# Hyena filters with a tile of taps per direction, and their transform taken from sums and differences

## The chip, the cores and the metric

The kernel runs on one core of a Trainium2 chip. The number that counts is the device time of one execution, in microseconds. The core has a matrix engine (TensorE, PE in the profile; PEld is its loading of weights), three engines for elementwise work (VectorE is DVE, ScalarE is ACT, GpSimd is POOL), and DMA queues, nearly all of which are issued here from SyncE (SP). Each engine works through its own list of instructions in order; semaphores tie the lists together.

## The reference, cut to what matters

The program is a two-layer backbone on 1024 latent tokens with 256 context tokens: an attention layer, then a layer of gated long convolutions (Hyena). All is float32. The change touches only the Fourier transforms of the convolution filters, which don't depend on the tokens:

```python
def hyena_filters(L, w1, b1, w2, b2, w3, b3, freq):
    ...
    hid = jnp.sin(_f32(freq) * (emb @ _f32(w1) + _f32(b1)))
    hid = jnp.sin(_f32(freq) * (hid @ _f32(w2) + _f32(b2)))
    h = (hid @ _f32(w3) + _f32(b3)).reshape(L, HY_ORDER, 2, HY_WIDTH)
    ...
    h = h * jnp.exp(-t * jnp.abs(deltas))[:, None, None, :]
    fwd, bwd = h[:, :, 0], h[:, :, 1]
    kern = jnp.concatenate([fwd, jnp.zeros((1, HY_ORDER, HY_WIDTH), jnp.float32), bwd[:0:-1]], axis=0)
    kern = kern / jnp.sum(jnp.abs(kern), axis=0, keepdims=True)
    return jnp.fft.rfft(kern, axis=0)
```

L is 1024, so a filter has 2048 taps: 1024 forward ones, a zero and 1023 backward ones. There are 2 orders of 1024 channels. A tap is a product of 64 hidden values with w3 and a bias b3, times a decay; a filter is divided by the sum of its absolute taps; its spectrum is wanted.

## The kernel before, in words

The filters are made in the first 250 us, ahead of and beside the preparation of the tokens. Channels are taken in 8 blocks (p) of 128, each with both orders, so 256 columns (CB). The 2048 taps of a block come in 16 tiles (g) of 128 rows, four tiles per step: `steps` lists 32 steps (p, gq), with gq from 3 down to 0, and one loop over n from 0 to 37 (line 605) issues, in this order:

- `taps(n)`, PE. A product in float32 is made of three in the faster fp32r form, with each factor split in a high and a low part (`mm3`, lines 100 to 103). For each of the four tiles, one matmul adds the bias (`ind` times `b4`, line 480) and three do the product of hidden values and w3 (`Hh`, `Hl` with `w3h`, `w3l`). The 64 hidden values of a forward row and of a backward row share the 128 rows of a tile, with zeros in the half that isn't theirs.
- `decay(n + 1)`, ACT: the decays of the next step (line 531).
- `second_stage`, PE (line 573): the second half of an earlier block's transform, in two halves, ps0 and ps1, each with `spectra` on DVE (line 584), which scales it by 1 / norm and sends it to DRAM (`Kd`). Tile `kc`, which it writes, has two buffers.
- `decayed(n)`, DVE (line 536): taps out of PSUM times decay into the tile `kern` of 128x1024 (two buffers).
- `first_stage(n - 1, j)`, j = 0 and 1: the first half of the transform, one float32 matmul of 128x512 on PE with the constant `FK` (line 558), and a copy by ACT into `aT` (line 560). So it works one step behind.
- `norms(n)`: ACT takes absolute values, in two pieces of 512 columns (line 545), and POOL adds them to `kacc` (line 547).
- `regroup`: four DMAs that turn `aT` into `au`, rows for the second stage.
- `split_coefs(p + 1)` once per block: w3 and b3 of the next block in high and low parts, by ACT, POOL and DVE (lines 336 to 345); `coefs` loads them.
- `pull(mods)`, `pull(stats)`, `pull(toks, 2)`: the work of other parts, threaded into the loop. Up to n = 11 `stats` gives ACT a square of a token tile (line 381). From n = 11 on `toks` prepares tokens: PE transposes four blocks (line 409), ACT scales them into `mraw` (line 414), DVE casts the high parts (line 421), POOL subtracts for the low parts (line 422), and in every second step DVE scales the next token tile `xt` (line 403).

This order is the order of each engine's list. PSUM is handed out by rotation: `pw` has two buffers for the taps, `pq` walks over three banks and from n = 20 over four, and whoever takes a bank waits for the reader of what was in it.

After n = 37 the input projection of the attention layer follows on the same engines.

Of the kernel before, what the change touches and what calls it, by code (L numbers as in the profile page):

```python
# [109 lines left out]
def backbone(tc, I, out):  # L110
# [200 lines left out]
    Hh = fp.tile([P, 16, P], F32R, tag="Hh", name="Hh")  # L311
    Hl = fp.tile([P, 16, P], F32R, tag="Hl", name="Hl")
    ind = fp.tile([P, P], F32R, tag="ind", name="ind")
    FKc = fp.tile([P, P], F32, tag="FK", name="FKc")
# [21 lines left out]
    def split_coefs(p):  # L336
        w3r, b3r, dl = coef[p]
        w3h = fp.tile([P, CB], F32R, tag="w3h", bufs=2, name=nm("w3h"))
        w3l = fp.tile([P, CB], F32R, tag="w3l", bufs=2, name=nm("w3l"))
        nc.scalar.copy(w3h, w3r)  # L340
# [2 lines left out]
        nc.scalar.copy(b4[0:2], b3r)
# [92 lines left out]
    with tc.manual_schedule(engines=ENG):  # L436
# [36 lines left out]
        def taps(n):  # L473
            p, gq = steps[n]
            w3h, w3l, b4, _ = coef[p]
            pws[n] = pw()
            for i in range(4):
                g = 4 * gq + i
                pv = pws[n][:, i * CB:(i + 1) * CB]
                nc.tensor.matmul(pv, ind, b4, start=True, stop=False)  # L480
# [1777 lines left out]
```

## Time and profile before

| | |
|---|---|
| median of 3 runs | 1850.01 us (1847.22 to 1852.31) |
| profiled execution | 1850.4 us, of which its span 1848.5 us |
| granted TensorE clock, mean | 0.986 |
| PE busy | 1744.1 us (94%) |
| DVE, ACT, POOL busy | 1136.7, 749.9, 866.2 us |
| `decayed(0)`, `decayed(12)`, `decayed(31)` start | 30.54, 100.50, 223.25 us |
| projection's first cast on ACT | 251.80 us |

The times of `decayed` on DVE (line 536) mark the steps of the loop, and are used as its milestones below: step n begins where `decayed(n)` starts. A row of the timeline gives the start, the time taken, the engine, the line, what is written and read, and how many instructions were put together; in brackets stands how long the engine was idle before it and what ended that. A group's row gives the total busy time and the mean of one in ns. A line's or tile's row gives the least, the median and the longest time of one.

### The profile page before, as it was taken

Reading aid. Unit: us, or ns where it says so; the run is one execution under the profiler, and the core shown is the slowest. Engines: PE = TensorE matmul, PEld = TensorE weight load, DVE = VectorE, ACT = ScalarE, POOL = GpSimd, SP = SyncE. Lnnn points to the kernel's source line nnn. Section 1 sums busy time; section 2 is a strip of 40 time slices with the busy share of each in tenths; the row PEclk is TensorE's granted clock in tenths of the full one; section 3 lists DMA queues with packets and bytes.
Section 4 is the critical chain, followed back from the end, with each engine's and each line's share of the span. In section 5 each row is a group of like instructions: output and inputs, shape, how many; then the busy total and the mean of one; then the engine's idle time right before and its main releaser. Section 6 shows DMA issues by size and latency. Waiting matters only on the chain.

```text
span 1848.5 us, 25379 instructions
## 1 busy us (share of the span) xinstructions
PE 1744.1 (94%) x9360; PEld 1332.5 (72%) x9360; DVE 1136.7 (61%) x1646; ACT 749.9 (41%) x1250; POOL 866.2 (47%) x606
## 2 busy tenths in 40 slices
PE   7899999999999998899999999999999999889898
PEld 2677788977765665565656688888878888778676
DVE  5467657446777877777777423555676666555743
ACT  4878711253544544343443333243333343333332
POOL 2457622443378778566666453234243334334300
PEclk9999999999999999899999999999999999999999
DMA  7776688122120011001000215567778787787623
GB/s 248 231 225 217 201 260 271 56 80 80 36 58 24 13 44 29 27 21 34 19 22 29 77 69 149 166 172 219 219 205 235 227 244 204 204 239 217 202 93 112
DMA packets 243427, 253.18 MB, mean 137 GB/s; under 512 B 28191, under 2 KB 193087, under 8 KB 242887
## 3 DMA queue, kind: packets, MB, share of 16 engines
q1 hardware_dynamic: 241128, 249.47, 45.2%
q10 hardware_dynamic: 2176, 2.10, 0.4%
q8 instruction: 74, 1.21, 0.3%
q14 instruction: 49, 0.40, 0.1%
HBM read 169.65 MB, written 61.94 MB: 125 GB/s over the span
## 4 chain that ended last, share of the span: by engine, by line
PE 54%; DVE 10%; DMA 5%; POOL 2%; ACT 2%; issue 2%; SPq 1%; POOLq 0%; DVEq 0%; ACTq 0%
PE pw L1253 8%; PE pw L103 8%; PE pw L101 8%; PE pw L102 8%; PE pv L1166 6%; PE pq L988 3%; PE pq L101 2%; PE pq L102 2%; PE pq L103 2%; PE pq L1818 2%; DMA K<-Kd 2%; PE pq L1835 2%; DVE mx L989 2%; DMA bd<-cbT 1%; DMA ad<-caT 1%
## 5 line engine op out<-in xcount | busy, mean ns | idle before, releaser
L1261 ACT ACTIVATE PT<-pw 128x1024 f32<-128x1024 f32 x160 | 163.6, 1023 | 218.2 <-PE pw L1253 210.1
L989 DVE TENSOR_REDUCE mx<-pq 128x1 f32<-128x512 f32 (+1 forms) x384 | 215.5, 594 | 42.3 <-PE pq L988 38.7
L101 PE MATMUL pw<-h1h,wh 128*128 128x512 f32 x512 | 209.6, 409 | 0.0
L103 PE MATMUL pw<-h1h,wl 128*128 128x512 f32 x512 | 202.5, 396 | 3.6 <-POOL wl L1676 3.6
L102 PE MATMUL pw<-h1l,wh 128*128 128x512 f32 x512 | 200.8, 392 | 0.0
L1811 POOL TENSOR_TENSOR K<-K,skp 128x512 f32<-128x512 f32 x64 | 85.4, 1336 | 217.7 <-DMA K<-Kd 210.9
L1175 POOL TENSOR_TENSOR acc<-acc,PT 128x1024 f32<-128x1024 f32 x62 | 147.7, 2383 | 35.9 <-ACT PT L1261 33.7
L103 PEld LDWEIGHTS pw<-h1h,wl 128*128 128x128 f32 x512 | 96.5, 188 | 25.7 <-POOL wl L1676 4.3
L1821 DVE SCALAR_TENSOR_TENSOR cB<-pq,K 64x512 f32<-64x512 f32 x64 | 44.3, 693 | 110.6 <-PE pq L1818 36.6
L547 POOL TENSOR_TENSOR kacc<-kacc,kabs 128x512 f32<-128x512 f32 x56 | 72.2, 1289 | 83.8 <-ACT kabs L545 81.9
L102 PEld LDWEIGHTS pw<-h1l,wh 128*128 128x128 f32 x512 | 97.3, 190 | 17.9
L101 PEld LDWEIGHTS pw<-h1h,wh 128*128 128x128 f32 x512 | 97.3, 190 | 17.5
L1173 POOL TENSOR_TENSOR acc<-PT,PT 128x1024 f32<-128x1024 f32 x31 | 73.7, 2377 | 74.3 <-DVE acs L1184 63.7
L1676 POOL TENSOR_TENSOR wl<-wr,wh 128x1024 fp32r<-128x1024 f32 x32 | 78.6, 2455 | 54.5 <-ACT wh L1675 36.2
L1791 ACT COPY caT<-pq 128x512 f32<-128x512 f32 x64 | 37.6, 587 | 142.0 <-PE pq L103 101.9
L1166 PE MATMUL pv<-PT,Va 128*64 128x256 f32 x640 | 86.7, 392 | 2.3 <-DVE gT L1212 2.3
L1166 PE MATMUL pv<-PT,Vm 128*64 128x256 f32 x640 | 85.9, 391 | 0.0
L1852 DVE TENSOR_TENSOR cil<-spare,cih 128x512 fp32r<-128x512 f32 x64 | 57.1, 930 | 42.2 <-ACT cih L1851 42.2
L573 PE MATMUL pq<-au,FBk 128*128 128x256 f32 x256 | 68.3, 391 | 11.8 <-DVE kc L584 11.6
L1818 PE MATMUL pq<-cau,FB 128*128 128x128 f32 x512 | 69.7, 280 | 8.9 <-DVE cA L1824 7.9
L1835 PEld LDWEIGHTS pq<-cA,GB 128*128 128x128 f32 x512 | 67.6, 193 | 12.3 <-issue 7.1
L1837 ACT COPY cbT<-pq 128x512 f32<-128x512 f32 x64 | 37.3, 587 | 95.9 <-PE pq L1835 53.0
(444 smaller groups left out, 4727.1 us busy)
## 6 DMA issues: line engine op xcount, KB each, us to landing
K<-Kd SPq DMA_DIRECT2D x128, 256.0 KB
au<-aT SPq DMA_DIRECT2D x128, 128.0 KB
space<-in_ada_w_dram SPq DMA_DIRECT2D x32, 512.0 KB
wr<-in_hy_w_in_dram SPq DMA_DIRECT2D x32, 512.0 KB
ad<-caT SPq DMA_DIRECT2D x64, 256.0 KB
cau<-ad SPq DMA_DIRECT2D x32, 512.0 KB
bd<-cbT SPq DMA_DIRECT2D x32, 512.0 KB
spare<-bd SPq DMA_DIRECT2D x64, 256.0 KB
```

The lines of the kernel that those rows point to most:

```text
L101: nc.tensor.matmul(ps, lh, rh, start=start, stop=False)
L102: nc.tensor.matmul(ps, lh, rl, start=False, stop=False)
L103: nc.tensor.matmul(ps, ll, rh, start=False, stop=stop)
L989: nc.vector.reduce_max(mxs[gi][:, p:p + 1], ps[:, :w], axis=AX.X)
L1166: nc.tensor.matmul(ps[64 * e:64 * e + 64, 0:256], vals[:, 2 * s + j], PT[:, j, 256 * e:256 * e + 256], start=s == 0 and j == 0, stop=s == ...
L1175: eng.tensor_tensor(accs[gi], accs[gi], PT, ALU.add)
L1253: nc.tensor.matmul(ps[:, 512 * j:512 * j + 512], l[:, kt * P:(kt + 1) * P], r, start=i == 0, stop=i == len(passes) - 1)
L1261: nc.scalar.activation(PT, ps.rearrange("p (a q) -> p a q", q=512), AF.Exp, scale=SC_A if kind == 0 else SC_M)
L1676: nc.gpsimd.tensor_tensor(wl, f(r), f(wh), ALU.subtract)
L1811: nc.gpsimd.tensor_tensor(K[:, 0], K[:, 0], B["skp"].unsqueeze(1).to_broadcast([P, 4, P]), ALU.add)
L1818: nc.tensor.matmul(ps[:, i * P:(i + 1) * P], FB[:, 4 * uc + i, :], au[:, 4 * (uc % 2) + i, :], start=True, stop=True)
L1835: nc.tensor.matmul(ps[:, i * P:(i + 1) * P], GB[:, 4 * uc + i, :], A1[:, i, :], start=True, stop=True)
```

## The change

A tile of taps now holds one direction: `HA` and `HB` are the stationary tiles for direction d and tile g. The 64 rows that held zeros hold the low parts of the hidden values (`HA`), and in `HB`, ones beside the high parts. On the other side `WA` has w3's high part twice, and `WB` w3's low part and the bias with its own low part. Two matmuls for a tile give all four products.

A step still has four tiles, two forward and two backward, so that `kern` has taps n in its first 512 columns and taps n + 1024 in its second 512. A new function `halves` makes their sum (a new tile `sum`, one buffer) and their difference (in place, in the first half), and `first_stage` transforms the sum with one constant matrix for the even frequencies and the difference with another for the odd ones. The numbers and sizes of the matmuls of the two transform stages and of the DMAs of `regroup` stay. `norms` comes in three pieces: two of 256 columns into `kabs` (one buffer now), and one of 512 in place in the second half of `kern`, after `halves` has read it. POOL adds in pieces of 256 columns, four per step. `split_coefs` has six ACT copies instead of two, two POOL subtractions and two DVE ones instead of one each, and stands at the third step of a block instead of the second.

```diff
     def split_coefs(p):
         w3r, b3r, dl = coef[p]
-        w3h = fp.tile([P, CB], F32R, tag="w3h", bufs=2, name=nm("w3h"))
-        w3l = fp.tile([P, CB], F32R, tag="w3l", bufs=2, name=nm("w3l"))
-        nc.scalar.copy(w3h, w3r)
-        nc.gpsimd.tensor_tensor(w3l, w3r, f(w3h), ALU.subtract)
-        b4 = b4s[p % 2]
-        nc.scalar.copy(b4[0:2], b3r)
-        nc.vector.tensor_tensor(b4[32:34], b3r, f(b4[0:2]), ALU.subtract)
+        wa = fp.tile([P, 2, CB], F32R, tag="WA", bufs=2, name=nm("WA"))
+        wb = WB[p % 2]
+        for i in range(2):
+            a = slice(64 * i, 64 * i + 64)
+            for h in (a, slice(64 - 64 * i, 128 - 64 * i)):
+                nc.scalar.copy(wa[h, i], w3r[a])
+            nc.gpsimd.tensor_tensor(wb[a, i], w3r[a], f(wa[a, i]), ALU.subtract)
+            b_ = 64 * (1 - i)
+            nc.scalar.copy(wb[b_:b_ + 1, i], b3r[b_:b_ + 1])
+            nc.vector.tensor_tensor(wb[b_ + 32:b_ + 33, i], b3r[b_:b_ + 1], f(wb[b_:b_ + 1, i]), ALU.subtract)
...
             for i in range(4):
-                g = 4 * gq + i
+                d, g = i // 2, 2 * gq + i % 2
                 pv = pws[n][:, i * CB:(i + 1) * CB]
-                nc.tensor.matmul(pv, ind, b4, start=True, stop=False)
-                mm3(nc, pv, Hh[:, g], Hl[:, g], w3h, w3l, False, True)
+                nc.tensor.matmul(pv, HA[:, d, g], wa[:, d], start=True, stop=False)
+                nc.tensor.matmul(pv, HB[:, d, g], wb[:, d], start=False, stop=True)
...
-            c = slice(8 * q, 8 * q + 8)
-            for h in hs:
-                nc.scalar.activation(Hr[h, c, h], args[q][h, :].rearrange("p (g m) -> p g m", m=64), AF.Sin)
-            nc.scalar.copy(Hh[:, c], Hr[:, c])
-            (nc.vector, nc.gpsimd)[q].tensor_tensor(Hl[:, c], Hr[:, c], f(Hh[:, c]), ALU.subtract)
+            c = slice(4 * q, 4 * q + 4)
+            a = args[q].rearrange("p (g m) -> p g m", m=P)
+            nc.scalar.activation(a, a, AF.Sin)
+            for d, h in enumerate(hs):
+                nc.scalar.copy(HA[h, d, c], a[h])
+                nc.gpsimd.tensor_copy(HB[h, d, c], HA[h, d, c])
+                nc.vector.tensor_tensor(HA[hs[1 - d], d, c], a[h], f(HA[h, d, c]), ALU.subtract)
...
-            for i in range(2):
-                ab = accs[p] if gq == 3 and i == 0 else fw.tile([P, 512], F32, tag="kabs", bufs=2, name=nm("kabs"))
-                nc.scalar.activation(ab, kns[n][:, 512 * i:512 * i + 512], AF.Abs)
-                if ab is not accs[p]:
-                    nc.gpsimd.tensor_tensor(accs[p], accs[p], ab, ALU.add)
...
+            if i == 2:
+                k = ab = kns[n][:, 512:]
+            else:
+                k = kns[n][:, CB * i:CB * i + CB]
+                ab = acc if first else fw.tile([P, CB], F32, tag="kabs", bufs=1, name=nm("kabs"))
+            nc.scalar.activation(ab, k, AF.Abs)
+            if not first:
+                for c in range(0, 512 if i == 2 else CB, CB):
+                    nc.gpsimd.tensor_tensor(acc, acc, ab[:, c:c + CB], ALU.add)
...
+        def halves(n):
+
+            a, b = kns[n][:, :512], kns[n][:, 512:]
+            t = fw.tile([P, 512], F32, tag="sum", bufs=1, name=nm("sum"))
+            nc.vector.tensor_tensor(t, a, b, ALU.add)
+            nc.vector.tensor_tensor(a, a, b, ALU.subtract)
+            sds[n] = t, a
...
-            nc.tensor.matmul(ps, FKc, kns[n][:, j * 512:(j + 1) * 512], start=True, stop=True)
+            nc.tensor.matmul(ps, FKc[:, j], sds[n][j], start=True, stop=True)
...
             if n < N:
                 decayed(n)
+                norms(n, 0)
             if n >= 6:
                 spectra(pb, ub, 0, ps0)
             if 0 < n <= N:
                 first_stage(n - 1, 0)
+            if n < N:
+                norms(n, 1)
+            if 0 < n <= N:
                 first_stage(n - 1, 1)
             if n < N:
-                norms(n)
+                halves(n)
+                norms(n, 2)
             if n >= 6:
                 ps1 = second_stage(pb, ub, 1)
...
-                if q == 1 and p + 1 < NT:
+                if q == 0 and p + 1 < NT:
+                    coefs(p + 1)
+                if q == 2 and p + 1 < NT:
                     split_coefs(p + 1)
-                if q == 2 and p + 2 < NT:
-                    coefs(p + 2)
```

How the lists move is shown for step 16, a step with tokens. On DVE, from `decayed(16)` to `decayed(17)`, it was (kern the taps, kc the spectra, hxh the cast tokens, xt the next token tile):

```order
L536 TENSOR_TENSOR kern_1233<-pw_1208,dec_1158 128x1024
L584 TENSOR_TENSOR kc_1235<-pq_1230,rn_1047 128x2x2x128
L584 TENSOR_TENSOR kc_1257<-pq_1249,rn_1047 128x2x2x128
L421 CAST hxh<-mraw_1265 128x4x128
L403 TENSOR_SCALAR xt_1139<-xt_1139,rr 128x1024
L536 TENSOR_TENSOR kern_1300<-pw_1275,dec_1225 128x1024
```

The same stretch of DVE's list now:

```order
L540 TENSOR_TENSOR kern_1206<-pw_1189,dec_1135 128x1024
L601 TENSOR_TENSOR kc_1210<-pq_1203,rn_1035 128x2x2x128
L566 TENSOR_TENSOR sum_1222<-kern_1206 128x512
L567 TENSOR_TENSOR kern_1206<-kern_1206 128x512
L601 TENSOR_TENSOR kc_1236<-pq_1228,rn_1035 128x2x2x128
L427 CAST hxh<-mraw_1250 128x4x128
L409 TENSOR_SCALAR xt_1124<-xt_1124,rr 128x1024
L540 TENSOR_TENSOR kern_1277<-pw_1260,dec_1198 128x1024
```

Sum and difference stand between the two spectra. On ACT, from the decays of step 17 to those of step 18, first as it was (aT is the first stage's output, mraw the scaled tokens):

```order
L531 ACTIVATE dec_1225<-dlt_874,tng 128x128 x4
L560 COPY aT_1021<-pq_1238 128x512
L560 COPY aT_1021<-pq_1241 128x512
L545 ACTIVATE kacc_1244<-kern_1233 128x512
L545 ACTIVATE kabs_1246<-kern_1233 128x512
L414 ACTIVATE mraw_1265<-pq_1260,shx_509,scx_510 128x128 x4
L531 ACTIVATE dec_1292<-dlt_874,tng 128x128 x4
```

and now:

```order
L535 ACTIVATE dec_1198<-dlt_976,tng 128x128 x4
L555 ACTIVATE kacc_1208<-kern_1206 128x256
L576 COPY aT_1006<-pq_1213 128x512
L555 ACTIVATE kabs_1216<-kern_1206 128x256
L576 COPY aT_1006<-pq_1219 128x512
L555 ACTIVATE kern_1206<-kern_1206 128x512
L420 ACTIVATE mraw_1250<-pq_1245,shx_509,scx_510 128x128 x4
L535 ACTIVATE dec_1269<-dlt_976,tng 128x128 x4
```

The absolute values are taken in three pieces, with the copies of the first stage between them, and the last piece, which writes into `kern`, still stands ahead of the tokens.

More of the change, by code (lines that the diff above doesn't have):

```diff
@@ L310, in backbone @@
     nwT = cp.tile([P, 2, NK], F32, tag="nwT", name="nwT")
[L311 to L314, printed above, removed]
+    HA = fp.tile([P, 2, NT, P], F32R, tag="HA", name="HA")
+    HB = fp.tile([P, 2, NT, P], F32R, tag="HB", name="HB")
+    FKc = fp.tile([P, 2, P], F32, tag="FK", name="FKc")
     FBk = fp.tile([P, 16, P], F32, tag="FBk", name="FBk")
@@ L317, in backbone @@
     CB = 256
-    b4s = [fp.tile([P, CB], F32R, tag=f"b4{i}", name=f"b4{i}") for i in range(2)]
-    for b4 in b4s:
-        nc.vector.memset(f(b4), 0.0)
+    WB = [fp.tile([P, 2, CB], F32R, tag=f"WB{i}", name=f"WB{i}") for i in range(2)]
+    for w in WB:
+        nc.vector.memset(f(w), 0.0)
+    nc.vector.memset(f(HB[64:128, 0]), 1.0)
+    nc.vector.memset(f(HB[0:64, 1]), 1.0)
     coef = {}
@@ L523, in backbone @@
         fw = fw_es.enter_context(pool("filtw", "right"))
-        aTs, accs, sums, rns, kns, aus = {}, {}, {}, {}, {}, {}
+        aTs, accs, sums, rns, kns, sds, aus = {}, {}, {}, {}, {}, {}, {}
         def decay(n):
@@ L537, in decayed, with norms @@
                                     decs.pop(n).unsqueeze(2).to_broadcast([P, 4, 2, P]), ALU.mult)
-        def norms(n):
+        def norms(n, i):
             p, gq = steps[n]
-            if gq == 3:
-                accs[p] = fw.tile([P, 512], F32, tag="kacc", bufs=1, name=nm("kacc"))
-            for i in range(2):
-                ab = accs[p] if gq == 3 and i == 0 else fw.tile([P, 512], F32, tag="kabs", bufs=2, name=nm("kabs"))
-                nc.scalar.activation(ab, kns[n][:, 512 * i:512 * i + 512], AF.Abs)
-                if ab is not accs[p]:
-                    nc.gpsimd.tensor_tensor(accs[p], accs[p], ab, ALU.add)
-            if gq == 0:
-                acc = accs.pop(p)
-                sums[p] = fw.tile([P, CB], F32, tag="ksum", bufs=1, name=nm("ksum"))
-                nc.gpsimd.tensor_tensor(sums[p], acc[:, :CB], acc[:, CB:], ALU.add)
+            first = gq == 3 and i == 0
+            if first:
+                accs[p] = fw.tile([P, CB], F32, tag="kacc", bufs=2, name=nm("kacc"))
+            acc = accs[p]
+            if i == 2:
[7 more added lines that the diff above has]
+                    nc.gpsimd.tensor_tensor(acc, acc, ab[:, c:c + CB], ALU.add)
+            if gq == 0 and i == 2:
+                sums[p] = accs.pop(p)
+        def halves(n):
[4 more added lines that the diff above has]
+            sds[n] = t, a
         def first_stage(n, j):
@@ L2179, in constants @@
     emb = np.concatenate([t[:, None].astype(np.float64), np.cos(ang), -np.sin(ang)], axis=1)
-    tneg = np.where(n == 1024, -1e30, -t[tok].astype(np.float64)).T
-    e = emb[tok]
-    emb2 = np.stack([e[:, :64].reshape(1024, 33), e[:, 64:].reshape(1024, 33)]).transpose(2, 0, 1)
+    tneg = np.where((d == 1) & (n == 0), -1e30, -t[tok].astype(np.float64)).reshape(16, P).T
+    emb2 = emb[tok].reshape(2, 1024, 33).transpose(2, 0, 1)
     lo, hi = np.log(1e-2) / 1.5, np.log(1e-2) / 0.3
     absd = np.abs(np.linspace(lo, hi, 1024))
-    ind = np.zeros((P, P))
-    for b in (0, 32):
-        ind[b, :64] = 1.0
-        ind[b + 1, 64:] = 1.0
     pos = (np.arange(8)[:, None] + 8 * np.arange(P)[None, :])
@@ L2204, in constants @@
     cK, sK = rope(32)
-    r = dict(FA=FA, FK=FK, FB=FB, FBk=FBk, GB=GB, IA=IA, emb=emb2, tneg=tneg, absd=absd, ind=ind,
+    r = dict(FA=FA, FK=FK, FB=FB, FBk=FBk, GB=GB, IA=IA, emb=emb2, tneg=tneg, absd=absd,
              cosA=cA.transpose(1, 0, 2), sinA=sA.transpose(1, 0, 2),
```

49 lines of the change are left out of this document (23 added, 26 removed).

## The prediction

> **What bounds the kernel now.** I read the busy times by stage first, with the stages cut at starts of `decayed`: steps 0 to 5, 6 to 11, and 12 to 30.
>
> ```profile
> core 0: us, PE busy (x) PEld busy (x) DVE busy (x) ACT busy (x) POOL busy (x), PEclk, DMA share, GB/s
> 30.50:61.60 31.10, 28.62 (x146) 18.53 (x142) 12.53 (x17) 24.48 (x60) 13.25 (x12) 0.95 0.68 224
> 61.60:100.50 38.90, 31.61 (x164) 23.72 (x164) 17.82 (x21) 29.40 (x66) 18.05 (x16) 1.00 0.79 245
> 100.50:223.25 122.75, 117.28 (x621) 89.42 (x620) 86.55 (x108) 93.76 (x237) 80.22 (x77) 0.99 0.67 213
> ```
>
> Steps 12 to 30, with the tokens, take 122.75 us for 19 steps, 6.46 each, and PE is busy for 117.28 of them (96%). Steps 6 to 11 take 6.48 each with PE at 81%, so something else paces them; in steps 0 to 5 ACT works for 24.48 us of 31.1. Next the timeline of PE in one token step (16):
>
> ```profile
> 123.37 0.36 PE L480 MATMUL pw<-b,ind 128*128 128x256 f32 x1
> ...
> 125.21 0.28 PE L103 MATMUL pw<-w3h,Hl 128*128 128x256 f32 x1
> 125.33 1.02 PE L573 MATMUL pq<-au,FBk 128*128 128x256 f32 x4
> 126.19 1.88 PE L558 MATMUL pq<-kern,FKc 128*128 128x512 f32 x4
> 128.07 1.13 PE L573 MATMUL pq<-au,FBk 128*128 128x256 f32 x4
> 129.04 0.60 PE L409 MATMUL pq<-ident,xt 128*128 128x128 f32 x4
> 129.39 0.36 PE L480 MATMUL pw<-b,ind 128*128 128x256 f32 x1
> ```
>
> The 16 matmuls of the taps run from 123.37 to 125.33, 1.96 us or 0.122 each; the transform stages and the transposes take the rest until 129.39, 6.02 in all without a gap. So token steps are paced by PE now. What DVE and then ACT do in step 16:
>
> ```profile
> 126.21 1.21 DVE L536 TENSOR_TENSOR kern<-pw,dec 128x1024 f32<-128x1024 f32 x1
> 127.34 0.67 DVE L584 TENSOR_TENSOR kc<-pq,rn 128x512 f32<-128x512 f32 x1
> 129.24 0.69 DVE L584 TENSOR_TENSOR kc<-pq,rn 128x512 f32<-128x512 f32 x1 [1.22 <-PE pq L573]
> 131.21 0.43 DVE L421 CAST hxh<-mraw 128x512 fp32r<-128x512 f32 x1 [1.28 <-ACT mraw L414]
> 131.56 0.74 DVE L403 TENSOR_SCALAR xt<-xt,rr 128x1024 f32<-128x1024 f32 x1
> 132.22 1.21 DVE L536 TENSOR_TENSOR kern<-pw,dec 128x1024 f32<-128x1024 f32 x1
> ```
>
> ```profile
> 128.59 0.63 ACT L545 ACTIVATE kacc<-kern 128x512 f32<-128x512 f32 x1
> 129.13 0.62 ACT L545 ACTIVATE kabs<-kern 128x512 f32<-128x512 f32 x1
> 129.68 1.50 ACT L414 ACTIVATE mraw<-pq,shx,scx 128x128 f32<-128x128 f32 x4
> 131.06 1.28 ACT L531 ACTIVATE dec<-dlt,tng 128x128 f32<-128x128 f32 x4
> ```
>
> In the first fence DVE has two gaps, 1.22 us before the second spectra, for PE, and 1.28 before the cast, for the scaled tokens. The second is a loop that PE's pace covers: `decayed` to absolute values to `mraw` to the cast to the next `decayed`, in which ACT and DVE stand in order.
>
> **The change part by part.**
>
> *Taps on PE.* 8 matmuls go per step: 8 x 0.122 = 0.98 us. PE's work in step 16 falls to 5.04, and over 19 steps by 18.6 us. This is a gain only where PE stays the last to finish.
>
> *The new loop in token steps.* `halves` needs 2 DVE instructions of 128x512 with both inputs in SBUF, and ACT's list makes a chain of it: the first absolute values, POOL's addition (since `kabs` now has one buffer, the second piece waits until POOL has read the first), the second absolute values, the difference (it overwrites what they read), the third piece (in place, after both), then the tokens' four `mraw`, the cast, and, in every second step, `xt`, before DVE can do the next `decayed`. Behind the difference on DVE stand the second spectra, whose bank PE wants back; behind the third piece on ACT stand `split_coefs`, `mraw` and the next decays, for which DVE waits, and PE two steps later, by the two `pw` buffers. The prices:
>
> ```profile
> L551 POOL TENSOR_TENSOR ksum<-kacc 128x256 f32<-128x256 f32 x8 | 6.0, 755 | 0.6
> L340 ACT CAST w3h<-w3r 128x256 fp32r<-128x256 f32 x8 | 3.2, 400 | 0.0
> L1184 DVE TENSOR_TENSOR acs<-acc x32: 671/680/1769, 505.0 to 1036.6; 128x512 f32<-128x512 f32 x32
> L421 DVE CAST h<-mraw x32: 279/432/1137, 138.4 to 231.3; 128x256 fp32r<-128x256 f32 x32
> L403 DVE TENSOR_SCALAR xt<-xt,rr x10: 742/1222/1359, 105.3 to 222.1; 128x1024 f32<-128x1024 f32 x10
> 129.89 1.29 POOL L547 TENSOR_TENSOR kacc<-kacc,kabs 128x512 f32<-128x512 f32 x1 [1.79 <-ACT kabs L545]
> ```
>
> `decayed` 1.21 (126.21 above). A first piece 0.40: absolute values of 256 columns don't occur, the nearest row is the cast of 128x256 at 400 ns. To POOL 0.14 (`kabs` ends at 129.13 + 0.62 = 129.75, POOL begins at 129.89). An addition of 128x256: 0.755, L551. The second piece 0.40. The difference 0.68, the median of a sum of the same size with both inputs in SBUF, L1184. The third piece holds ACT for 0.55 (129.13 to 129.68 above), `mraw` 1.50, the last cast 0.28 at its least and 0.43 at its median. Hand-overs between ACT, DVE and POOL apart from the 0.14: 0.03 from `mraw` to the cast (129.68 + 1.50 = 131.18 to 131.21), five of them 0.15. Sum without `xt`: 1.21 + 0.40 + 0.14 + 0.755 + 0.40 + 0.68 + 0.55 + 1.50 + 0.15 = 5.79, with the cast 6.07 to 6.22. `xt` adds 0.74 to 1.22, least and median; between them, without a nearer row, I take 0.98. That makes 6.81 at the least (6.07 + 0.74) and 7.20 as I take it (6.22 + 0.98). The first half of the chain, up to the difference, hides the sum and both first-stage copies; the decays of the next step (1.28, 131.06 above) run beside `xt` and `decayed`.
>
> Corrections over the 19 steps: 5 of them are first steps of a block, without the first addition, and save 0.14 + 0.755 less what is left of a copy, say 0.57 each: -2.9. Four hold `split_coefs`, six ACT copies ahead of `mraw`:
>
> ```profile
> 60.28 0.40 ACT L340 CAST w3h<-w3r 128x256 fp32r<-128x256 f32 x1
> 60.57 0.40 ACT L343 CAST b<-b3r 2x256 fp32r<-2x256 f32 x1
> L648 DVE RECIPROCAL rn<-pq 128x256 f32<-128x256 f32 x8 | 14.1, 1758 | 1.6 <-PE pq L636 0.9
> ```
>
> Copies follow each other after 0.29, so six are 1.8 us, 4 x 1.8 = +7.2. They were two, 0.6, and had PE's pace as cover. In five steps the reciprocal, 1.76 us on DVE, stands behind the second spectra, which now come after the difference; of it I count 0.6 each as sticking out before the cast, +3.0. Nine steps without and ten with `xt` (of the 10 in L403): 9 x 6.22 + 10 x 7.20 - 2.9 + 7.2 + 3.0 = 135.3, against 122.75: **+12.5 us**. Low end: 9 x 6.07 + 10 x 6.81 - 2.9 + 7.2 = 127.0, with the reciprocals hidden, +4. For the high end collisions have to be priced:
>
> ```profile
> 502.53 0.69 DVE L1178 TENSOR_TENSOR acc<-acc,PT 128x512 f32<-128x512 f32 x1
> ...
> 518.05 1.37 DVE L1178 TENSOR_TENSOR acc<-acc,PT 128x512 f32<-128x512 f32 x1
> ```
>
> ```profile
> 517.59 1.27 POOL L1228 TENSOR_TENSOR gT<-gT,rb 64x512 f32<-64x512 f32 x1 [0.34 <-DMA rb<-rd]
> ```
>
> L1178 is a sum of two SBUF inputs of the size of the new ones. At 502.53 it takes 0.69; at 518.05 it begins under a POOL instruction that runs until 517.59 + 1.27 = 518.86, and takes 1.37, to 519.42: it starts about when POOL ends. So sum, difference, cast and `xt` each can lose up to one addition of 0.755 to POOL, and POOL the like. In the loop one such loss per step is +0.75 x 19 = 14 us, half of them 7: high end +12.5 + 14 = +27.
>
> The Trainium skill (SBUF — State Buffer, § Who interferes with whom) says the same as a rule: a DVE instruction with two SBUF inputs and a GpSimd one that reads SBUF exclude each other for their whole length. The trace agrees, with 1.37 against 0.69 us; the rule speaks against this change, which puts both kinds in the same stretch, and as a bound of its own is the last rival.
>
> *Steps 1 to 5.* ACT's list sets them, without a gap, as its timeline shows:
>
> ```profile
> 45.78 1.15 ACT L545 ACTIVATE kabs<-kern 128x512 f32<-128x512 f32 x2
> ...
> 49.04 1.03 ACT L560 COPY aT<-pq 128x512 f32<-128x512 f32 x2
> 49.98 1.15 ACT L545 ACTIVATE kabs<-kern 128x512 f32<-128x512 f32 x2
> ```
>
> The absolute values of two steps are 4.20 us apart, and two first-stage copies hold it 0.94 (49.04 to 49.98), 0.47 each. The chain adds to each step the wait of the second piece for POOL's addition, 0.14 + 0.755 + 0.05 less the copy beside it, 0.47, and of the third for the difference, 0.68 + 0.06 less a copy, 0.27; with the extra instruction 0.8. That is 4.0 in five steps, and 0.6 for more split copies, less those that leave the stretch. Before that PE does `taps(1)`, slowly:
>
> ```profile
> 35.78 0.58 PE L480 MATMUL pw<-b,ind 128*128 128x256 f32 x1
> 38.56 1.88 PE L558 MATMUL pq<-kern,FKc 128*128 128x512 f32 x4
> ```
>
> 35.78 to 38.56 for 16, of which half, 1.4, comes back. Together +3.2; between -1.4 (if POOL and DVE answer inside the copies) and +6.
>
> *Steps 6 to 11.* The spectra wait for `kc`, a buffer whose DMA isn't done:
>
> ```profile
> 69.50 0.69 DVE L584 TENSOR_TENSOR kc<-pq,rn 128x512 f32<-128x512 f32 x1 [1.69 <-DMA Kd<-kc]
> 76.01 0.69 DVE L584 TENSOR_TENSOR kc<-pq,rn 128x512 f32<-128x512 f32 x1 [1.40 <-DMA Kd<-kc]
> ```
>
> The two are 6.51 us apart, the step. `regroup` and the spectra move the same bytes in the same number of DMAs, so PE's 0.98 is worth nothing here; the new instructions are covered, if closely: ACT is busy for 29.40 of 38.90 us and gets 6 x 0.8 more, and 3.0 for two sets of split copies in place of one small one, 37.2. 0; if the cover fails, +3.
>
> *The rest.* In the beginning, sines and copies change within stretches that wait for the DMAs of the weights: 0. After step 31, `sum` is ready 1.21 + 0.69 + 0.68 us after `decayed(31)`, before PE gets to it: 0. What follows takes its place in the lists, and moves as a block. The loads of w3 and b3 now come two steps (13 us at 6.46) ahead of their split, into buffers freed two steps before: 0; a late one would hold ACT, at the cost of its lateness.
>
> Sum: 12.5 + 3.2 = 15.7. From the profiled execution's 1850.4 us (span 1848.5; 0.4 above the median of the runs shown): 1866, said as **1866 us**.
>
> **The rivals.**
>
> *PE still sets the pace, faster.* The loop is hidden, if ACT and DVE in fact overlap pieces that I put in a row. Then token steps lose 0.98 each, 18.6, and steps 1 to 5 some 2: 1830. For it: PE at 96%, DVE at 86.55 of 122.75 us. Against it: the chain, free of every collision, is already longer than a PE step of 5.04. Half of this gain would give 1840. 0.12 together.
>
> *Even.* The chain at its least (+4) and steps 1 to 5 at -1.4: 1853; with a few hand-overs hidden 1850. 0.15.
>
> *POOL and DVE exclude each other all through.* Per block POOL has 15 additions of 0.755, 2 splits and 8 token subtractions of about the same, 18.9 us; DVE has 8 sums and differences of 0.68, 8 casts of 0.28, 2 `xt` of 0.74, 9.2: 28.1 for 4 steps, 7.0 a step, against 6.46. Alone that gives 19 x 7.0 = 133, about my sum; as losses inside the chain, one per step, +27, with +3 to +6 in steps 1 to 5: 1880 to 1883. 0.20. This is the place where it would be decided: the sum that begins beside the first addition, and the casts beside the last two.
>
> *The change does not do what it says*: left out, as the order shows 256 taps matmuls for 512 and two DVE instructions more per step.
>
> **How the numbers follow.** My forecast, a loop over ACT, POOL and DVE that sets the token steps at about 7.1 us: 0.53. Range: low from even's upper part, 1852, high from the collisions, 1883; left out are the faster rival and some of even. A change under 0.3% (5.5 us) can't be told from none in a measurement of this kernel. Faster by over that: 0.12; within: 0.14; slower: 0.74.
>
> **What would show it.** Right: token steps of 6.8 to 7.6 us between starts of `decayed`; PE busy for 75 to 85% there, its longest waits for banks or for ACT and DVE; the difference waiting for ACT, the third absolute values for the difference, and `mraw` not for PE. Steps 6 to 11 unchanged at 6.5, with waits for the `Kd` DMAs. Steps 1 to 5 at about 5 us. Sums and differences well over 0.68 us in the mean show the collisions. Wrong: token steps under 6.4 with PE still at 95%, or the loss at another place, in the last steps' DMAs or in the projection behind them.

## The result and the profile after

The changed kernel took 1871.8 us in the median of 4 runs (1866.7 to 1873.1), against 1848.6 for the kernel before beside it: a ratio of 1.012, 95% interval 1.009 to 1.015. Predicted were 1866, in a range of 1852 to 1883. Its profiled execution took 1870.59 us, with a span of 1868.8. The busy times by stage of the changed kernel, cut as before at the starts of `decayed(0)`, `(6)`, `(12)` and `(31)` (`decayed` is now line 540):

```profile
core 0: us, PE busy (x) PEld busy (x) DVE busy (x) ACT busy (x) POOL busy (x), PEclk, DMA share, GB/s
28.88:63.93 35.05, 24.32 (x96) 13.05 (x92) 20.00 (x29) 27.37 (x68) 20.73 (x23) 0.90 0.71 219
63.93:103.19 39.26, 31.17 (x121) 21.56 (x122) 26.88 (x38) 32.69 (x81) 24.48 (x28) 0.91 0.77 232
103.19:246.81 143.62, 113.77 (x470) 77.44 (x468) 104.00 (x152) 104.46 (x272) 105.72 (x115) 0.90 0.62 183
```

| stretch | before | after | difference | predicted |
|---|---|---|---|---|
| up to `decayed(0)` | 30.54 | 28.88 | -1.7 | 0 |
| steps 0 to 5 | 31.05 | 35.05 | +4.0 | +3.2 |
| steps 6 to 11 | 38.91 | 39.26 | +0.4 | 0 |
| steps 12 to 30 | 122.75 | 143.62 | **+20.9** | **+12.5** |
| `decayed(31)` to the projection's cast | 28.55 | 27.40 | -1.2 | 0 |
| the rest of the span | 1596.7 | 1594.6 | -2.1 | 0 |

The loss lies in the token steps, 7.56 us each where they were 6.46. PE, busy for 96% of them before, is now busy for 79%. In a token step with a split of the coefficients (18), DVE, ACT and POOL do this:

```profile
145.74 1.22 DVE L540 TENSOR_TENSOR kern<-pw,dec 128x1024 f32<-128x1024 f32 x1
146.87 0.68 DVE L601 TENSOR_TENSOR kc<-pq,rn 128x512 f32<-128x512 f32 x1
147.47 0.68 DVE L566 TENSOR_TENSOR sum<-kern 128x512 f32<-128x512 f32 x1
149.22 0.69 DVE L567 TENSOR_TENSOR kern<-kern 128x512 f32<-128x512 f32 x1 [1.07 <-ACT kabs L555]
149.83 0.68 DVE L601 TENSOR_TENSOR kc<-pq,rn 128x512 f32<-128x512 f32 x1
151.76 0.77 DVE L350 TENSOR_TENSOR WB<-b3r,WB 1x256 fp32r<-1x256 f32 x1 [1.24 <-ACT WB L349]
152.92 0.47 DVE L350 TENSOR_TENSOR WB<-b3r,WB 1x256 fp32r<-1x256 f32 x1 [0.39 <-ACT WB L349]
153.61 0.51 DVE L427 CAST h<-mraw 128x256 fp32r<-128x256 f32 x1 [0.23 <-ACT mraw L420]
154.30 0.85 DVE L427 CAST h<-mraw 128x256 fp32r<-128x256 f32 x1 [0.17 <-ACT mraw L420]
155.07 0.74 DVE L409 TENSOR_SCALAR xt<-xt,rr 128x1024 f32<-128x1024 f32 x1
155.73 1.21 DVE L540 TENSOR_TENSOR kern<-pw,dec 128x1024 f32<-128x1024 f32 x1
```

```profile
147.05 0.42 ACT L555 ACTIVATE kabs<-kern 128x256 f32<-128x256 f32 x1 [0.81 <-DVE kern L540]
148.77 0.42 ACT L555 ACTIVATE kabs<-kern 128x256 f32<-128x256 f32 x1 [0.83 <-POOL kacc L558]
149.94 0.63 ACT L555 ACTIVATE kern<-kern 128x512 f32<-128x512 f32 x1 [0.28 <-DVE kern L567]
150.48 0.81 ACT L346 CAST WA<-w3r 64x256 fp32r<-64x256 f32 x2
151.32 0.40 ACT L349 CAST WB<-b3r 1x256 fp32r<-1x256 f32 x1
151.63 0.82 ACT L346 CAST WA<-w3r 64x256 fp32r<-64x256 f32 x2
152.48 0.40 ACT L349 CAST WB<-b3r 1x256 fp32r<-1x256 f32 x1
152.79 1.47 ACT L420 ACTIVATE mraw<-pq,shl,scl 128x128 f32<-128x128 f32 x4
```

```profile
147.61 1.12 POOL L558 TENSOR_TENSOR kacc<-kacc,kabs 128x256 f32<-128x256 f32 x1 [0.48 <-ACT kabs L555]
149.27 1.24 POOL L558 TENSOR_TENSOR kacc<-kacc,kabs 128x256 f32<-128x256 f32 x1 [0.53 <-ACT kabs L555]
```

The chain of the prediction can be followed from row to row: `decayed` ends, 147.05 first absolute values, 147.61 POOL's addition, 148.77 second absolute values, 149.22 difference, 149.94 third piece, then the copies of the split, 152.79 `mraw`, casts, `xt`, and at 155.73 the next `decayed`. Every link waits for the one before it (in the brackets). Only two lengths are new: the addition takes 1.12 us, and the copies 2.31 (150.48 to 152.79). The waits of steps 12 to 30 (total, how often, the longest) show two of the links in nearly every step, and the groups give the means:

```profile
DVE kern L567 <- ACT kabs L555: 17.2, 17, 2.6
ACT kern L555 <- DVE kern L567: 5.3, 19, 0.3
```

```profile
L558 POOL TENSOR_TENSOR kacc<-kacc,kabs 128x256 f32<-128x256 f32 x33 | 39.3, 1191 | 27.1 <-ACT kabs L555 27.1
L558 POOL TENSOR_TENSOR kacc<-kacc,kern 128x256 f32<-128x256 f32 x38 | 28.0, 737 | 5.6 <-ACT kern L555 4.1
L566 DVE TENSOR_TENSOR sum<-kern 128x512 f32<-128x512 f32 x19 | 13.2, 697 | 0.3 <-PE pq L575 0.3
L567 DVE TENSOR_TENSOR kern<-kern 128x512 f32<-128x512 f32 x19 | 13.2, 693 | 17.4 <-ACT kabs L555 17.2
```

The same addition of 128x256 takes 737 ns on the third piece, when DVE does neither sum nor difference, and 1191 on the first two, which begin under them. Sum and difference keep their 0.69 to 0.70: they start first, and POOL is the one held up.

### The profile page after: what moved, and what is told of

Same layout as the page of the kernel before. It is cut to its first block, busy times and chain, and to the rows that moved or that the text cites. A ratio compares the mean times of both kernels' runs of the same rounds, so it can differ in the third digit from the quotient of the medians.

```text
span 1868.8 us, 25190 instructions
## 1 busy us (share of the span) xinstructions
PE 1736.6 (93%) x9104; PEld 1313.2 (70%) x9104; DVE 1177.1 (63%) x1723; ACT 768.4 (41%) x1313; POOL 905.2 (48%) x672
## 4 chain that ended last, share of the span: by engine, by line
PE 53%; DVE 10%; DMA 5%; POOL 2%; issue 2%; ACT 1%; SPq 1%; DVEq 0%; POOLq 0%; ACTq 0%
PE pw L1274 8%; PE pw L103 8%; PE pw L101 8%; PE pw L102 8%; PE pv L1187 6%; DMA K<-Kd 3%; PE pq L1009 3%; PE pq L101 2%; PE pq L102 2%; PE pq L103 2%; PE pq L1839 2%; PE pq L1856 2%; DVE mx L1010 2%; DVE acc L1199 1%; DVE cil L1873 1%
## 5 line engine op out<-in xcount | busy, mean ns | idle before, releaser
L1282 ACT ACTIVATE PT<-pw 128x1024 f32<-128x1024 f32 x160 | 163.7, 1024 | 220.8 <-PE pw L1274 211.2
L590 PE MATMUL pq<-au,FBk 128*128 128x256 f32 x256 | 75.0, 423 | 22.8 <-DVE kc L601 14.2
L558 POOL TENSOR_TENSOR kacc<-kacc,kabs 128x256 f32<-128x256 f32 x56 | 63.6, 1137 | 54.1 <-ACT kabs L555 54.1
L590 PEld LDWEIGHTS pq<-au,FBk 128*128 128x128 f32 x256 | 49.7, 209 | 47.0 <-DVE kc L601 24.8
```

Source lines behind the costliest of these rows:

```text
L590: nc.tensor.matmul(ps[:, i * CB:(i + 1) * CB], FBk[:, 4 * uc + 2 * j + i, :], aus[p, uc][:, 2 * j + i, :], start=True, stop=True)
L1282: nc.scalar.activation(PT, ps.rearrange("p (a q) -> p a q", q=512), AF.Exp, scale=SC_A if kind == 0 else SC_M)
```

## The experiments

In all of them the measure is the stretch from `decayed(12)` to `decayed(31)`, 122.75 us before and 143.62 after, as each profile shows it. What follows the projection's cast differs by up to 20 us between the single executions of these kernels (1587.4 to 1607.4 us) without a change there, so the total of one execution says little about this stretch.

| | steps 12 to 30 | total, us |
|---|---|---|
| before / after | 122.75 / 143.62 | 1848.6 / 1871.8 |
| b1_halves (before, plus sum and difference) | 124.98 | 1848.0, one run |
| p1_half_taps (before, half of PE's taps) | 116.30 | 1845.9, one run |
| e5_taps_twice | 144.81 | 1883.0, one run |
| e1_no_first_add | 134.03 | 1869.5, one run |
| f1_abs_dec | 136.11 | 1850.5, one run |
| e2_split_late | 141.46 | 1873.2, one run |
| n1_no_split | 133.38 | 1853.0, one run |
| g1_all | 131.78 | ratio 1.004 (1.000 to 1.008) |
| g2_early / g3_early_spec | 143.80 / 137.92 | 1874.5, one run / 1.0105 (1.005 to 1.016) |
| g6_low_spec | 127.40 | 1.0005 (0.998 to 1.003) |
| g7_act_loads | 127.19 | 1.002 (1.000 to 1.005) |

**Is PE still the pace? (e5_taps_twice)**

```diff
-                nc.tensor.matmul(pv, HA[:, d, g], wa[:, d], start=True, stop=False)
-                nc.tensor.matmul(pv, HB[:, d, g], wb[:, d], start=False, stop=True)
+                for _ in range(2):
+                    nc.tensor.matmul(pv, HA[:, d, g], wa[:, d], start=True, stop=False)
+                    nc.tensor.matmul(pv, HB[:, d, g], wb[:, d], start=False, stop=True)
```

> The changed kernel, with each pair of taps matmuls done twice (the second pair overwrites the first), so PE does as many taps matmuls as before the change, 16 per step. Chain theory (absolute values, POOL's addition, difference, third absolute values, mraw, cast, decayed set the token steps): PE's work per token step goes from 5.1 to 6.1 us and stays under the step of 7.56, so decayed(12) to decayed(31) stays at 143.6 us, +0 to +3, and the time at 0 to +5 us. Rival, PE's work still sets the steps: +0.98 us in each of 32 steps, +19 us between decayed(12) and decayed(31).

The stretch of this kernel, and its busy times:

```profile
104.02:248.83 144.81, 127.23 (x626) 95.37 (x624) 103.84 (x152) 104.45 (x272) 106.08 (x115) 0.93 0.61 180
```

PE got eight matmuls more per step (626 recorded in place of 470) and 13.5 us more busy time; the stretch grew by 1.2. PE does not set the stretch any more.

**Are sum and difference dear by themselves? (b1_halves)** The kernel before, with the two DVE instructions put in, writing to a tile that is no longer needed; nobody waits for them.

```diff
...
+                o_ = decs.pop(n).rearrange("p g c -> p (g c)")
+                nc.vector.tensor_tensor(o_, kns[n][:, :512], kns[n][:, 512:], ALU.add)
+                nc.vector.tensor_tensor(o_, kns[n][:, :512], kns[n][:, 512:], ALU.subtract)
                 norms(n)
```

> The kernel before, with two more DVE instructions per step: sum and difference of the halves of kern, written one after the other into the used-up decay tile and read by nobody, in the place that halves has in the change. Chain theory: they fit in DVE's gap of 1.22 us ahead of the second spectra, nothing waits for them, and decayed(12) to decayed(31) goes from 122.75 to 123 to 127 us. Rival, DVE's and POOL's instructions with two SBUF inputs exclude each other and that is what costs: one collision of about 0.6 us per step, +8 to +14 us there.

124.98, +2.2. They meet POOL's additions there too: the sum takes about 0.75 us and the difference 0.98 in place of 0.69. But nobody waits for them, and the 8 to 14 us of the rival do not come. As work they nearly fit; it is their place in the chain that costs.

**What would PE's gain have been without the chain? (p1_half_taps)**

```diff
-                mm3(nc, pv, Hh[:, g], Hl[:, g], w3h, w3l, False, True)
+                nc.tensor.matmul(pv, Hh[:, g], w3h, start=False, stop=True)
```

> The kernel before with 2 matmuls a slice for the taps instead of 4: the products with the low parts are left out, everything else stays, so only PE's share of the change is done (the values are less exact). PE's work per token step falls from 6.02 to 5.04 us. If PE alone set the 6.46 us of a token step, as the prediction said, steps 12 to 31 fall from 122.75 by up to 18.6, to 104 to 110 us, or to the bytes: 213 GB/s times 6.46 us is 1.38 MB a step, at the 245 GB/s that steps 6 to 11 reached 5.6 us a step, 107 us. Rival: ACT, DVE and the DMA of the spectra stood close behind PE, so that less than half of it comes back: 114 us or more.

```profile
94.30:210.60 116.30, 101.14 (x469) 69.33 (x469) 82.99 (x109) 96.27 (x238) 81.31 (x79) 1.00 0.74 233
```

And its waits in a part of that stretch (100 to 205 us):

```profile
DVE kc L584 <- PE pq L573: 10.7, 10, 1.9
PEld pq L573 <- DVE kc L584: 10.4, 6, 2.3
DVE h L421 <- ACT mraw L414: 9.0, 14, 1.0
PEld pq L409 <- DVE kc L584: 8.6, 6, 3.3
```

PE's share alone brings 6.45 us of the 18.6 that its matmuls get shorter: the rival was right. PE and DVE now wait for each other at the spectra, and DVE for the scaled tokens. So PE at 96% was no proof that all of its time could be had; ACT and DVE stood about 0.34 us a step behind it (6.45 / 19).

**POOL's addition (e1_no_first_add, f1_abs_dec).** The first leaves the addition of the first piece out:

```diff
-            if not first:
+            if not first and i:
                 for c in range(0, 512 if i == 2 else CB, CB):
```

> The changed kernel without POOL's addition of the first piece of absolute values (the sums are incomplete, so the rms of the filters is wrong and only the time counts). The second piece then waits for nothing. Theory: POOL's addition, 1.19 us in the mean, because it is held up by DVE's sum, lies in the chain of the 14 token steps that have it. The chain gets shorter by 0.14 + 1.19 less the 0.47 of a first-stage copy beside it, 0.86 us each: steps 12 to 31 at 131.6 us, between 129 and 134. With POOL's addition at the 0.755 that was predicted it would be 0.42 each: about 137.7. Rival: the steps are set elsewhere (copies of the split, tokens); no change within 2 us.

134.03, at the upper edge of what was expected: -9.6. The 14 steps that have this addition got 0.78 us shorter in the mean, the five without it 0.26 longer. An addition of 0.755 us would have given 0.42 a step (137.7), one with the collision 0.86, and this is the nearer price. The second keeps the work but takes the wait away: 512 absolute values in one piece, written into the tile of decays, which `decayed` has read; nothing waits for POOL.

```diff
...
-                k = kns[n][:, CB * i:CB * i + CB]
-                ab = acc if first else fw.tile([P, CB], F32, tag="kabs", bufs=1, name=nm("kabs"))
+                k = kns[n][:, :512]
+                ab = decs.pop(n).rearrange("p g c -> p (g c)")
...
```

> The changed kernel, with the absolute values of the first half taken in one piece of 512 columns into the used-up decay tile of the step, so that no piece waits for POOL's addition; POOL still adds four pieces of 256. Chain theory: 0.8 us of waiting goes in 14 of the 19 token steps, and the extra ACT instruction: -9 to -14 us between decayed(12) and decayed(31), so 130 to 135 us, and steps 1 to 5 some 2 us faster. Rival, POOL and DVE exclude each other all through: the same instructions remain, so -4 us at most.

136.11, -7.5, short of the 9 to 14 that were expected, and more than the rival's 4. Two groups of this kernel (104 to 225 us) tell why not more:

```profile
L560 POOL TENSOR_TENSOR kacc<-kacc,dec 128x256 f32<-128x256 f32 x26 | 26.2, 1009 | 11.6 <-ACT dec L555 10.5
L569 DVE TENSOR_TENSOR kern<-kern 128x512 f32<-128x512 f32 x17 | 17.6, 1037 | 1.8
```

Without the wait POOL's two additions run on under the difference, and now the difference is the one held up, at 1.04 us instead of 0.69. The collision did not go, it changed sides.

**The split (e2_split_late, n1_no_split).** The first moves it behind the tokens on ACT:

```diff
-                if q == 2 and p + 1 < NT:
-                    split_coefs(p + 1)
...
                 pull(toks, 2)
+            if n < N and q == 2 and p + 1 < NT:
+                split_coefs(p + 1)
```

> The changed kernel, with split_coefs issued behind the tokens' part of the step instead of ahead of it. Chain theory: mraw no longer waits for its six ACT copies (2.3 us a block in the trace of the change), of which about 1 us comes back since the next step's decays and absolute values now stand behind them: -4 to -9 us between decayed(12) and decayed(31), so 135 to 140 us. Rival, the token steps are bound by the shared work of POOL and DVE: under 2 us, since no work goes.

A miss: 141.46, only -2.2, and the split steps still took about 9.6 us; steps 6 to 11 even grew, from 39.26 to 43.16. Its timeline shows the same copies now ahead of the next decays, and DVE's two subtractions for the biases, which wait for them, ahead of the next `decayed`. It was not the place on one list; the work stood in a ring. So the second leaves the work out, from the third block on:

```diff
         w3r, b3r, dl = coef[p]
+        if p > 1:
+            coef[p] = *coef[p - 2][:2], dl
+            return
```

> The changed kernel without the splitting of the coefficients from the third block on: later blocks use the split taps of the block two before, so their filters are wrong and only the time counts. The loads of w3 and b3 stay. Steps 12 to 31 took 143.6 us in the changed kernel, and the four steps that hold a split 9.55 to 10.02 each. Theory: the six ACT copies (2.31 us each time) and the scaled tokens, casts and decayed taps queued behind them set those steps. Then these steps fall to about 7, as the others, and steps 12 to 31 take 131 to 135 us; by the 1.8 us a split that the prediction counted, 136.4. Rival: the long steps come from the reciprocal in the step before, behind which PE and the spectra are late; then steps 12 to 31 fall by less than 5 us.

```profile
98.11:231.49 133.38, 104.78 (x466) 69.15 (x466) 98.35 (x144) 94.97 (x248) 97.99 (x107) 0.99 0.66 196
```

133.38, -10.2: the four splits cost 2.6 us each, 2.3 of it in the step that holds the split, not the 1.8 of the prediction. That is half of the stretch's loss of 20.9; the chain without them is the other 10.6. Steps 6 to 11, which had two splits, fell too, from 39.26 to 33.84 us.

**Versions without the chain (g1_all to g7_act_loads).** g1_all is f1_abs_dec with the third piece and the split behind the tokens, w3 loaded twice so that one ACT copy of 128x512 does for four, and the biases' low parts on POOL:

```diff
-            for h in (a, slice(64 - 64 * i, 128 - 64 * i)):
-                nc.scalar.copy(wa[h, i], w3r[a])
+        nc.scalar.copy(wa, w3r)
...
-            nc.vector.tensor_tensor(wb[b_ + 32:b_ + 33, i], b3r[b_:b_ + 1], f(wb[b_:b_ + 1, i]), ALU.subtract)
+            nc.gpsimd.tensor_tensor(wb[b_ + 32:b_ + 33, i], b3r[b_:b_ + 1], f(wb[b_:b_ + 1, i]), ALU.subtract)
...
                 pull(toks, 2)
+            if n < N:
+                norms(n, 2)
+            if n < N and q == 2 and p + 1 < NT:
+                split_coefs(p + 1)
```

> A version meant to keep the gain and leave out the loop: the first 512 absolute values go in one piece into the used tile of decays, so that no piece waits for POOL; the third piece and the split come behind the tokens on ACT; w3 is loaded twice so that one ACT copy of 128x512 takes the place of four of 64x256, and the low parts of the biases go to POOL. Theory of the loop over ACT, POOL and DVE: mraw no longer waits for the difference, and token steps take what the busiest engine needs, PE 5.1, ACT 5.1, DVE about 5.6 (decayed 1.21, two spectra 1.2, sum and difference 1.5, two casts 0.7, half an xt, a quarter of a reciprocal): 5.8 to 6.4 each, steps 12 to 31 at 110 to 121 us, and the whole 4 to 14 us under the kernel before. Rival: collisions of POOL and DVE set the pace (28.1 us of work in turns for four steps, 7.0 a step): steps 12 to 31 at 133 or more, the whole not faster than before.

131.78: 12 us less, but far from 110 to 121. The two steps behind each split took 6.9 to 8.5, all others but two 6.2 to 6.6, and behind the split PE waited for the biases' low parts, which stand behind POOL's other work:

```profile
122.59 0.39 PE L487 MATMUL pw<-WB,HB 128*128 128x256 f32 x1 [1.98 <-POOL WB L352]
```

g2_early is g1_all with the split a step earlier, POOL's bias part a step behind it and the loads moved (below in part, against g1_all); g3_early_spec also puts the first spectra ahead of `decayed`.

```diff
...
-            if n < N and q == 2 and p + 1 < NT:
+            if n < N and q == 1 and p + 1 < NT:
                 split_coefs(p + 1)
+            if n < N and q == 2 and p + 1 < NT:
+                bias_low(p + 1)
+            if n < N and q == 2 and p + 2 < NT:
+                coefs(p + 2)
```

> As the version with all three edits (g1_all), but the coefficients are split one step earlier, POOL's low parts of the biases come a step after the rest, and the loads stand two steps ahead as in the kernel before. In g1_all the steps with a split and those after them took 7.2 to 8.5 us, because PE waited 1.98 us for POOL's low parts of the biases. Theory: what is left of the excess there is lateness of the split, not its work. Then no PE wait for them remains and steps 12 to 31 fall from 131.8 to 123 to 127 us. Rival: POOL is full (its additions at 0.94 instead of 0.75 under DVE's sums and differences), so that the split's 3.5 us on POOL come out as time wherever they stand: 130 or more.

> As g2_early, and the first spectra of a step stand ahead of the decayed taps on DVE instead of behind them. In g1_all the second transform's matmuls wait 0.93 us in each step for that spectra to free a bank, and the transposes, the scaled tokens and the cast, for which DVE then idles 0.9 to 1.2 us, stand behind them. Theory of the loop over PE, ACT and DVE: DVE's idle time before the casts goes, and steps take DVE's own work, 5.6 to 5.9 us: steps 12 to 31 at 107 to 115 us, the whole 8 to 16 us under the kernel before. Rival: POOL and DVE in turns, 7.0 us a step, or POOL full: no better than g2_early within 3 us, the whole within 1% of the kernel before.

Both missed, at 143.80 and 137.92. The waits of g2_early in this stretch name a queue that I had not counted, SP's:

```profile
SPq L333 <- POOL WB L349: 10.7, 3, 5.0
SPq L335 <- POOL WB L359: 7.5, 3, 3.7
DVE kc L612 <- DMA Kd<-kc: 11.1, 6, 3.8
```

L333 loads w3 over what POOL's split still reads, and SP's later entries, the stores of the spectra among them, stand behind it; DVE then waits 11.1 us for those stores. g6_low_spec is g3_early_spec with the loads where the changed kernel has them and the biases' low parts on DVE; g7_act_loads lets ACT issue the loads (both in part, first g6_low_spec, then g7_act_loads):

```diff
...
                 decayed(n)
                 norms(n, 0)
+                if q == 2 and p + 1 < NT:
+                    bias_low(p + 1)
```

```diff
...
+            if n < N and q == 3 and p + 2 < NT:
+                coefs(p + 2, nc.scalar)
```

> From the version g1_all: the split stands one step earlier (its loads stay where they are), the low parts of the biases are taken on DVE a step later, behind the decayed taps, where they wait for nothing and PE does not need them for two steps, and the first spectra of a step stand ahead of the decayed taps. In g2_early and g3_early_spec PE still waited 0.60 us for POOL's low parts, and DVE up to 2.60 us for the DMA of the spectra, whose queue had the loads in it. Theory: with the split's lateness gone, and the loads out of the spectra's way, steps take 6.1 to 6.4 us as the others of g1_all: steps 12 to 31 at 116 to 122 us, the whole 0 to 10 us under the kernel before. Rival: ACT, DVE and POOL, each over 75% busy and bound to one another at every piece, make up elsewhere what is taken away here: 126 or more, not faster than before.

> As g6_low_spec, but the loads of the coefficients from the third block on are issued by ACT at the fourth step of a block, behind its decays, instead of by SP. In g6_low_spec SP waits 7.9 us in three times, up to 3.8 each, for POOL's split before it may load w3 over it, with the stores of the spectra and the loads of the second stage behind it, and DVE waits up to 2.32 us for those stores. Theory: that is what is left of the excess at the split; the waits for the spectra's stores go, and steps 12 to 31 fall from 127.4 to 121 to 125 us, the whole within 5 us of the kernel before or up to 5 under it. Rival: the stores are late for another reason (bytes: 216 GB/s in these steps, and the engines' own loop); no change within 2 us in the steps, and the whole like g6_low_spec.

The stretch of g6_low_spec and DVE's groups in it, then a part of that of g7_act_loads (100 to 225 us) and a group of ACT there:

```profile
98.02:225.42 127.40, 107.08 (x467) 72.46 (x466) 114.04 (x152) 96.84 (x241) 100.18 (x115) 0.96 0.73 216
```

```profile
L577 DVE TENSOR_TENSOR sum<-kern 128x512 f32<-128x512 f32 x19 | 16.2, 853 | 1.7
L578 DVE TENSOR_TENSOR kern<-kern 128x512 f32<-128x512 f32 x19 | 19.3, 1018 | 2.8 <-ACT dec L564 0.9
```

```profile
100.00:225.00 125.00, 101.74 (x449) 67.75 (x449) 112.89 (x147) 96.08 (x238) 97.49 (x113) 0.99 0.73 213
```

```profile
L544 ACT ACTIVATE dec<-dlt,tng 128x128 f32<-128x128 f32 x76 | 24.3, 396 | 7.9 <-DMA b3r<-in_b_dram 3.2 <-POOL kacc L569 3.1 <-DMA au<-aT 1.6
```

In g7_act_loads SP's waits for POOL's split are gone, DVE waits 0.4 us for the stores in place of 3.0, and the steps are no shorter: 127.19. The rival of g6_low_spec holds. Of the rival of g7_act_loads only the number holds: the stores are no longer late, but ACT, which now issues the loads, is held 3.2 us by them itself (`b3r` in its group). DVE is now busy for 90% (112.89 of 125.00 us; before 86.55 of 122.75), and 35.5 us of that in g6_low_spec are sums and differences, 0.85 and 1.02 us each. With the chain taken apart the added DVE work, stretched by POOL, is by its busy time the likeliest next bound, at 6.7 us a step; no run took it away, so that is not shown. The best version, g6_low_spec, equals the kernel before; none beats it.

## Why the prediction was right, and where it was not

*The token steps.* The chain, its order and its hand-overs were as predicted: the difference waits for ACT 17 times of 19, the third piece for the difference, `mraw` never for PE in the waits listed, PE is busy for 79% (75 to 85 were given), the mean step 7.56 (6.8 to 7.6). The sizes were not; by kinds of step:

| steps | predicted each | measured each | surplus in all |
|---|---|---|---|
| with a split: 14, 18, 22, 26 | 6.22 + 0.98 + 1.8 = 9.00 | 9.89 | +3.6 |
| with a reciprocal: 13, 17, ... 29 | 6.22 + 0.6 = 6.82 | 7.24 | +2.1 |
| 15, 19, 23, 27 | 6.22 | 6.62 | +1.6 |
| first of a block: 12, 16, ... 28 | 7.20 - 0.57 = 6.63 | 6.72 | +0.5 |
| 30 | 7.20 | 7.73 | +0.5 |

Together 8.3 us, the difference between 12.5 and 20.9 (to rounding). Two terms were too small, one was missing and one was too large:

- POOL's addition: 0.755 in the sum. The first additions, the ones on the chain, took 1.12 to 1.20 us (1.15 in the mean, without step 25), since they begin under DVE's sum. The prediction had this as a collision that either engine could lose, but for the high end only, and the sign it gave for it was slower sums and differences, which did not come (0.69 to 0.70). In the central sum it had been left at nothing, though the place was named. With it the plain steps 15, 19, 23 and 27 come out: 6.22 + 0.40 = 6.62.
- The split: the two copies of 64 rows take 0.84 us together (150.48 to 151.32), 0.42 each and not 0.29, and a bias copy 0.31, so six make 2.31 and not 1.8; behind them comes a cast of 0.85 us beside POOL's subtraction for the tokens. In n1_no_split these steps are 2.3 us shorter, so 9.00 + 0.40 + 0.5 = 9.9.
- One step was overlooked: at the end of step 24 ACT and then POOL split a piece of w_in (`w`, lines 686 and 687). POOL is held by it for 3.52 us, and the chain now runs through POOL. Step 25 took 8.71 us instead of 6.9:

```profile
198.53 1.43 ACT L686 CAST w<-w 128x288 fp32r<-128x288 f32 x4
...
200.76 3.52 POOL L687 TENSOR_TENSOR w<-w,w 128x288 fp32r<-128x288 f32 x4
...
205.00 0.42 ACT L555 ACTIVATE kabs<-kern 128x256 f32<-128x256 f32 x1 [2.63 <-POOL kacc L558]
```

- The reciprocals' 0.6 was too large. Steps 13, 17, 21 and 29 took 6.88 in the mean, close to the predicted 6.82, but only because two errors cancel: they have POOL's addition too, and are 0.26 longer than the plain steps.

`xt` had been taken at 0.98 and measured 0.93. The first steps of blocks fit in the mean alone (5.42 to 7.55).

*Steps 0 to 5*: +4.0 us for 3.2 predicted. Steps 1 to 5 took 5.8 us in the mean, where about 5 had been given, and not evenly: 9.71 for step 2, which holds a split. Steps 0 to 5 of b1_halves took 28.52 us where the kernel before took 31.05, so single executions tell no more here. *Steps 6 to 11*: +0.4 for 0 predicted, but for another reason. The prediction had the stores of the spectra pace them whatever PE does. p1_half_taps did them in 34.12 us and n1_no_split, which has the chain and lacks the two splits, in 33.84, so they were not bound at 6.5 us a step: PE's gain was real there, and the two splits took it back. Two errors cancelled, which is luck.

*The whole.* The span of the profiled execution grew by 20.3 us, the median by 23.2, for 15.7 predicted. The token steps alone missed by 8.4; the stretches ahead of `decayed(0)` and behind `decayed(31)`, predicted at 0, gave 5.0 back. No run explains that part, and the end differs by more between single executions; that the total came nearer than its main term is luck.

*The rivals.* "PE still sets the pace, faster" falls with e5_taps_twice, and p1_half_taps shows that its 1830 us was out of reach even without a chain. "Even" falls with the result. "POOL and DVE exclude each other all through" (1880 to 1883) did not come: in the changed kernel the first additions lost 0.40 us each, while sums and differences kept their 0.69 to 0.70 in the mean; DVE's casts and `xt` took longer in some steps (0.87 and 1.22 us at the most, 0.30 and 0.75 in the median). It may be what is left in g6_low_spec and g7_act_loads. The Trainium skill (SBUF — State Buffer, § Who interferes with whom) has it that whoever issues first keeps the shared port and the other blocks. The trace agrees: POOL loses in the changed kernel, where the sum starts 0.14 us ahead of the addition (1191 ns for 737), and DVE in f1_abs_dec, where POOL's two additions run on under the difference (1037 for 693).

## What to carry to other kernels

An engine that is busy for 96% of a stage bounds it, but what can be won there is the distance to the next one: halving PE's taps alone was worth 6.5 of 18.6 us. Before work is moved to other engines, write down the ring that it closes in the lists (here DVE, ACT, POOL, DVE, ACT, DVE in one step), price each link as it runs beside its neighbours and not alone, and walk every other thing that stands in those lists, once per block or once per program. A collision for a port that is named as a risk belongs in the central sum when the order of the lists makes the two meet in every step.
